# Low parts of weight units: by an accumulating DMA in place of a VectorE subtraction

## The chip, the cores and the metric

The kernel runs on one core of one Trainium2 chip. The metric is the device time of one execution in microseconds; times that a profile shows are microseconds from the start of the profiled execution's span.

## The reference, cut to what matters

Two layers of a bidirectional encoder over 1024 tokens of 1024 channels, in float32. Each layer norms its input, multiplies it by one input projection `w_in`, feeds the pieces to four mixers (Fourier, convolution, dilated attention, pooling), gates and projects each mixer's output, weights it by a sigmoid gate that is computed from the normed input, sums the four, and projects the sum by `w_out`.

```python
def hybrid_layer(x, ...):
    h = rms_norm(x, norm_g)
    z = h @ w_in                                   # 1024 x 4352
    u_a, u_b, u_c, u_d, u_gate = split(z)
    gate_paths = silu(u_gate)                      # one per mixer
    branch_outs = (fourier_mix(u_a, w_fourier), conformer_conv(u_b, ...),
                   dilated_mixture(u_c, cos, sin), multiscale_pool(u_d, ...))
    merged = 0
    for n, y in enumerate(branch_outs):
        y_n = (y * gate_paths[:, :, n]) @ w_branch[n]
        merged = merged + sigmoid(h @ w_gate[n] + b_gate[n]) * y_n
    return x + merged @ w_out
# out = rms_norm(layer 1(layer 0(x)))
```

## The kernel before

All activations lie transposed, channels on 128 partitions and tokens along the free axis, in two halves of 512 tokens. TensorE takes float32 operands rounded to a shorter format (`F32R`) in one pass, so every operand is split into a high and a low part, hi + lo = x exactly, and each product is the sum of three passes: hi hi, hi lo, lo hi (`passes`, L122; `together`, L249, where several units of weights share the right operand). A sum in PSUM takes its passes in order, so the third pass of its first block needs the low part of the weights.

Weights come in units of 1024 x 128 (512 KB). `load_unit` (L107) takes a raw place from the pool `wr` (L119, `raw`, two places for the whole kernel, the gate weights included), has SP load the unit into it, and calls `split` (L102): ScalarE copies the raw unit to the rounded high part (L104), VectorE subtracts that from the raw unit and writes the low part (L105). Both parts have places of their own: six halves under the tag `w`, which is three units, or places that are kept (tags `H` and `M`). The loads have a raised priority (`AHEAD` = 100 instructions), so that they run ahead of the products as far as places are free. A raw place is free again when both readers are done with it.

`load_unit` is called 135 times: for 75 units of `w_in` (attention, gate paths, mixers' inputs; `in_unit`, L325, with two halves of 24 products each; `begin`, L257, which in the first layer takes up to eight units at the start for one half of the tokens and loads some of them again later), 32 of `w_out` (`out_proj`, L1079), 16 of `w_branch` (`branch`, L922), and four each of `w_pool`, `w_pw` and `dft` in side work that is interleaved with the main products. The last layer's `out_proj` runs over the tokens in a half and two quarters: eight units for the half, eight for the third quarter (three of them loaded as kept copies during the half, five loaded then), and the last quarter with the kept eight.

`split` is also used for activations (`h`, attention probabilities, mixers' outputs) and, by `weight_form` (L961), for the gate weights' forms in the gate stages (`gates`, L1000), which don't call `load_unit`.

Instructions on each engine and each queue run in the order in which the tile framework's scheduler placed them when the program was built. SP issues nearly all DMAs: unit loads, the stores of branch products, the rotations' partition swaps in `rope_unit` (L353), the loads of x. POOL's queue issues the loads of branch products in the gate stages (L985) and the stores of merged blocks (L1062), and POOL does a few memsets.

Of the kernel before, what the change touches and what calls it, by code (L numbers as in the profile page):

```python
# [14 lines left out]
P = 128  # L15
# [23 lines left out]
# columns of the packed per-layer parameters  # L39
C_G, C_CW, C_CB, C_LG, C_LB, C_PS, C_BG, C_N = 0, 8, 70, 72, 74, 76, 78, 110  # L40
# columns of the packed constants
# [4 lines left out]
class Net:  # L46
# [41 lines left out]
    def half_pair(self, name, tag):  # L88
        """hi and lo of one [P, H] operand."""
        t = self.slot(name, F32R, tag=tag)  # L90
        return t[:, 0:H], t[:, H:S]
# [10 lines left out]
    def split(self, hi, lo, src):  # L102
        """hi + lo = src exactly, each part with few enough bits for one pass."""
        self.nc.scalar.activation(out=hi, in_=src, func=AF.Copy)  # L104
        self.nc.vector.tensor_tensor(out=lo, in0=src, in1=hi.bitcast(F32), op=ALU.subtract)  # L105

    def load_unit(self, src, kc=KC, n=P, tag=None, ahead=AHEAD):  # L107
        """A right shape of weights: hi and lo."""
# [5 lines left out]
        with self.tc.high_priority(offset=ahead):  # L114
            self.nc.sync.dma_start(out=flat, in_=src)
            self.split(*out, flat)
        return out

# [3 lines left out]
    def passes(self, ps, pairs, main=False, first=True, open_=False):  # L122
        """ps = sum over pairs of (lhsT hi, lo), (rhs hi, lo), in float32 by three passes.
        Not first: added to what ps holds. open_: ps is read between sums that add up in it."""
# [8 lines left out]
    def gemm(self, ps, w, x, hf, main=True):  # L133
        """x[k][hf]: hi and lo of the k-th 128 rows of the right operand, one half of the tokens."""
        self.passes(ps, [((w[0][:, k], w[1][:, k]), xk[hf]) for k, xk in enumerate(x)], main)

# [31 lines left out]
    def tok_stat(self, chunks, ones, name):  # L168
        """PSUM [token, 4 tiles, 2]: the mean over channels of the given [P, H] chunks' columns."""
# [24 lines left out]
    def spread(self, st, name):  # L194
        """[token, 4 tiles] to PSUM [P, H], the same in every partition."""
# [53 lines left out]
    def together(self, ws, xs, pss, ks=range(KC)):  # L249
        """Products that share their right operands."""  # L250
# [6 lines left out]
    def begin(self, units):  # L257
        """The first layer's first units. For the first of them and the first half of the tokens, x g is divided
        by the norms of its tokens after the products, which need not wait for them."""
# [70 lines left out]
    def first_units(self, l, units):  # L330
        """Their first halves of the tokens before the second ones, whose norm is still under way."""
# [8 lines left out]
    def perm_dst(self, ap, g, hf):  # L340
        """Where the tokens of half hf lie in group g's order."""
# [11 lines left out]
    def rope_unit(self, l, u, g, cos, sin, q):  # L353
        """The rotated unit, split and stacked, for each of the two heads (a: rows 0:64, b: rows 64:128).
        For k: hi over lo (a), lo over hi (b). For q: hi twice (a, b), and lo, both heads."""
# [40 lines left out]
    def v_tiles(self, vt, g, where):  # L396
        """v in the group's token order, tokens on partitions: hi, lo, rows by key offset."""
# [30 lines left out]
    def att_tiles(self, l, hp, g, q, k, vt, done):  # L428
# [18 lines left out]
        def products(t):  # L447
            # one bank per head: the two heads' products run in different rows of the array
# [70 lines left out]
        # scores of one tile, the transposes of the one before, the weighted sums of the one before that  # L519
# [30 lines left out]
    def att_mix(self, groups, park):  # L550
        """The groups' outputs weighted by the softmax of their log-sum-exps, parked in DRAM."""
# [72 lines left out]
    def pool_windows(self, c, up):  # L624
        """In place of u: its centred window mean less u."""
# [21 lines left out]
    def pool_mix(self, l, ups, gps, park):  # L647
        """The gated pooling branch, parked in DRAM until its merge."""
# [37 lines left out]
    def fourier_in(self, l, c):  # L686
        """The tokens folded twice, split. With a[n] = u[n] + u[S-n], s[n] = u[n] - u[S-n] and h = S/2, for n < S/4:
        a[n] + a[h-n] | a[n] - a[h-n] for the even and odd cosines, s[n] - s[h-n] | s[n] + s[h-n] for the sines.
        Aside: a[S/4], and the sum over all of u with alternating signs."""
# [35 lines left out]
    def fourier_pq(self, l, us, res):  # L725
        """P and Q: the transform over the channels and w_fourier, in one product each."""
# [72 lines left out]
    def gate_later(self, ys, gps, park):  # L799
        """The two chunks times their gate paths, once both are there, parked in DRAM."""  # L800
# [8 lines left out]
    def conv_units(self, l, c):  # L809
        """a times sigmoid(g), into DRAM between zeros."""  # L810
# [35 lines left out]
    def conv_mix(self, l, hf, gps, park):  # L846
        """Layer norm, SiLU, w_pw and the gate path of one half of the tokens, parked in DRAM."""
# [50 lines left out]
    def gated(self, load, gps, out):  # L898
        """Split halves of the two gated [P, S] chunks."""
# [34 lines left out]
    def token_forms(self, out):  # L934
        """The sums of h's blocks (b11 | b12 / b21 | b22: channels by tokens) for seven products in place of eight."""
# [30 lines left out]
    def spare(self, flip):  # L966
        """One more place for weights, two by turns."""
# [3 lines left out]
    def weight_forms(self, l):  # L971
        """In the order of the products: the weights' forms of all pairs of blocks, and what their merge needs."""
# [27 lines left out]
    def gates(self, l, tf):  # L1000
        """merged = sum over n of sigmoid(w_gate_n h + b_n) y_n, for two blocks of 128 channels at a time."""
# [263 lines left out]
```

## Time and profile before

| | us |
|---|---|
| median of 3 runs | 2097.05 (2096.38 to 2097.84) |
| span of the profiled execution | 2096.5 |
| what lies around the span, taken as the difference to the median | 0.55 |
| TensorE busy | 2023.1 |
| VectorE busy | 1487.6 |
| ScalarE busy | 1100.2 |
| POOL busy | 41.3 |

No time of the profiled execution is given apart from its span. In the profile PE is TensorE's products and PEld its loads of weights, which overlap; DVE is VectorE, ACT ScalarE, POOL GpSimd, and SPq and POOLq are the queues on which these two issue DMAs. A line such as L105 is that of `split`, whoever called it, so groups are told apart by the names of their tiles: `w<-wr` are the units of `load_unit`, `wf` the gate weights' forms. Idle time of an engine costs nothing by itself; what counts is which wait ends last in a stretch.

### The profile page before, as it was taken

The numbers are of one execution on the slowest core, as the hardware profiler recorded it, in microseconds if no ns is written. First come the engines' busy times: TensorE is split into PE (matmuls) and PEld (weight loads), VectorE is DVE, ScalarE is ACT, GpSimd is POOL, SyncE is SP. The second block draws the span as 40 slices with busy tenths as digits, with TensorE's granted clock in tenths as the row PEclk, the third lists the DMA queues.
The fourth block names the chain that finished last, engine by engine and source line by source line (L and its number), as shares of the span: only waits on it lengthen the run. The fifth ranks groups of instructions, "written<-read, shape, count | busy, mean of one in ns | idle before, by whom it ended". The sixth has DMA issues, their size and how long they took to land.

```text
span 2096.5 us, 26763 instructions
## 1 busy us (share of the span) xinstructions
PE 2023.1 (96%) x9500; PEld 1645.9 (79%) x9500; DVE 1487.6 (71%) x2752; ACT 1100.2 (52%) x2025; POOL 41.3 (2%) x90
## 2 busy tenths in 40 slices
PE   8998898999999999999999998989999999999998
PEld 6776686778878888887888776867888888888888
DVE  7596777775657877877655867687555867777775
ACT  7347666657755433434321566666685744344451
POOL 0000000000000000000000000000000000000000
PEclk9999998999999999999999999999999999999999
DMA  6231122212586234236421321223127843243443
GB/s 229 81 106 58 49 82 62 96 41 81 190 284 235 86 136 141 100 112 245 158 85 49 106 65 52 77 71 101 46 87 266 278 159 125 97 141 131 144 167 101
DMA packets 122438, 257.81 MB, mean 123 GB/s; under 512 B 31808, under 2 KB 36544, under 8 KB 122304
## 3 DMA queue, kind: packets, MB, share of 16 engines
q1 hardware_dynamic: 111360, 216.25, 31.1%
q0 software_dynamic: 10944, 39.85, 5.6%
q8 instruction: 75, 1.23, 0.2%
q14 instruction: 59, 0.48, 0.1%
HBM read 176.16 MB, written 67.30 MB: 116 GB/s over the span
## 4 chain that ended last, share of the span: by engine, by line
PE 73%; DVE 10%; ACT 9%; DMA 4%; issue 3%; SPq 1%; DVEq 0%; ACTq 0%
PE z L128 20%; PE ga L128 12%; PE g L128 8%; PE gb L128 8%; PE py L128 8%; PE op L128 6%; PE z L255 3%; DVE cv L841 2%; PE pv L128 2%; PE pt L486 1%; ACT p L474 1%; DVE w L105 1%; ACT qa L377 1%; ACT ql L383 1%; ACT qb L375 1%
## 5 line engine op out<-in xcount | busy, mean ns | idle before, releaser
L128 PE MATMUL z<-h,w 128*128 128x512 f32 x3000 | 760.9, 404 | 1.4 <-DVE gp L604 1.4
L128 PEld LDWEIGHTS z<-h,w 128*128 128x128 f32 x3000 | 557.0, 192 | 119.5 <-DVE gp L604 1.8
L104 ACT ACTIVATE w<-wr 128x1024 fp32r<-128x1024 f32 (+1 forms) x135 | 137.8, 1022 | 185.9 <-PE z L128 80.2
L105 DVE TENSOR_TENSOR w<-wr,w 128x1024 fp32r<-128x1024 f32 (+1 forms) x135 | 158.9, 1179 | 97.8 <-ACT w L104 81.6
L128 PE MATMUL ga<-t,wf 128*128 128x512 f32 x768 | 188.9, 395 | 0.0
L128 PE MATMUL gb<-t,wf 128*128 128x512 f32 x768 | 187.4, 393 | 0.0
L128 PE MATMUL g<-h,wf 128*128 128x512 f32 x768 | 186.3, 391 | 0.0
L128 PE MATMUL op<-m,w 128*128 128x512 f32 (+1 forms) x960 | 181.3, 349 | 2.0 <-DVE m L105 1.9
L128 PE MATMUL py<-g,w 128*128 128x512 f32 x768 | 181.5, 395 | 0.5 <-ACT y L930 0.5
L841 DVE SCALAR_TENSOR_TENSOR cv<-cv,params 128x512 f32<-128x512 f32 x240 | 178.9, 745 | 2.2
L128 PEld LDWEIGHTS op<-m,w 128*128 128x128 f32 x960 | 153.6, 189 | 28.0 <-DVE m L105 3.5
L128 PEld LDWEIGHTS ga<-t,wf 128*128 128x128 f32 x768 | 144.3, 188 | 33.6
L128 PEld LDWEIGHTS py<-g,w 128*128 128x128 f32 x768 | 143.3, 188 | 34.3 <-ACT y L930 1.7
L128 PEld LDWEIGHTS gb<-t,wf 128*128 128x128 f32 x768 | 144.3, 188 | 32.9
L128 PEld LDWEIGHTS g<-h,wf 128*128 128x128 f32 x768 | 144.2, 188 | 31.9
L104 ACT ACTIVATE wf<-wr 128x512 fp32r<-128x512 f32 x144 | 90.9, 632 | 130.4 <-issue 48.4
L105 DVE TENSOR_TENSOR wf<-wr,wf 128x512 fp32r<-128x512 f32 x144 | 98.8, 686 | 21.5 <-ACT wf L104 20.3
L474 ACT ACTIVATE p<-p,nm 128x192 f32<-128x192 f32 (+2 forms) x192 | 84.4, 441 | 54.0 <-DVE nm L471 53.6
L105 DVE TENSOR_TENSOR pl<-pt,ph 128x256 fp32r<-128x256 f32 (+2 forms) x136 | 63.2, 465 | 54.1 <-ACT ph L104 53.8
L104 ACT ACTIVATE wf<-s 128x512 fp32r<-128x512 f32 x64 | 40.4, 632 | 107.3 <-PE gb L128 64.4
L128 PE MATMUL ga<-h,wf 128*128 128x512 f32 x384 | 93.5, 392 | 0.0
L128 PEld LDWEIGHTS ga<-h,wf 128*128 128x128 f32 x384 | 72.1, 188 | 16.4
(246 smaller groups left out, 2832.4 us busy)
## 6 DMA issues: line engine op xcount, KB each, us to landing
wr<-in_w_in_dram SPq DMA_DIRECT2D x75, 512.0 KB, 3.7
y<-y SPq DMA_DIRECT2D x128, 256.0 KB, 3.8
y<-y POOLq DMA_DIRECT2D x64, 512.0 KB, 4.8
wr<-in_w_gate_dram SPq DMA_DIRECT2D x48, 512.0 KB, 4.4
wr<-in_w_out_dram SPq DMA_DIRECT2D x32, 512.0 KB, 3.6
rot<-rt SPq DMA_DIRECT2D x192, 64.0 KB, 2.0
cv<-in_w_gate_dram SPq DMA_DIRECT2D x16, 512.0 KB, 5.1
wr<-in_w_branch_dram SPq DMA_DIRECT2D x16, 512.0 KB, 5.0
```

The lines of the kernel that those rows point to most:

```text
L104: self.nc.scalar.activation(out=hi, in_=src, func=AF.Copy)
L105: self.nc.vector.tensor_tensor(out=lo, in0=src, in1=hi.bitcast(F32), op=ALU.subtract)
L128: self.nc.tensor.matmul(ps, w, x, start=(first and i + u == 0), stop=(i == n - 1 and u == 2), skip_group_check=open_)
L255: self.nc.tensor.matmul(ps, a[:, k], b, start=(k + j == 0), stop=(k == KC - 1 and j == 2))
L375: nc.scalar.activation(out=dst(x, own), in_=src(own), func=AF.Copy)
L377: nc.scalar.activation(out=dst(x, other), in_=src(own), func=AF.Copy)
L383: nc.scalar.activation(out=dst(xl, al), in_=src(al), func=AF.Copy)
L474: nc.scalar.activation(out=ph, in_=ph, func=AF.Exp, bias=nm[:, h:h + 1], accum_out=st[:, t, 2 + h:3 + h])
L486: nc.tensor.transpose(pt[:rows[ci], cs], p[:, off:off + rows[ci]], self.ident)
L841: self.tc.keep_in_program_order(nc.vector.scalar_tensor_tensor(out=y, in0=u[:, j:j + H], scalar=tap(j), in1=y, op0=ALU.mult, op1=ALU.add))
```

## The change

`load_unit` no longer calls `split`, but a new function. ScalarE copies the raw unit times -1, rounded, into the place of the low part. POOL issues a DMA that reads the raw unit and adds it to what stands in that place, so that it holds raw minus rounded raw. ScalarE copies the raw unit once more, into the high part. VectorE has no part in it. The order in the code is: negated copy, DMA, copy. All callers of `load_unit` are concerned, not only those of `w_in` and `w_out`; the other users of `split` are as before. The rest of the diff takes comments out.

```diff
         with self.tc.high_priority(offset=ahead):
             self.nc.sync.dma_start(out=flat, in_=src)
-            self.split(*out, flat)
+            self.split_by_dma(*out, flat)
         return out
+
+    def split_by_dma(self, hi, lo, src):
+
+        self.nc.scalar.activation(out=lo, in_=src, func=AF.Copy, scale=-1.0)
+        self.nc.gpsimd.dma_start(out=lo, in_=src, accum_op=ALU.add)
+        self.nc.scalar.activation(out=hi, in_=src, func=AF.Copy)
```

## Rows read from the trace of the kernel before

**Rows 1.** page, totals: busy us of each engine, share of the span, instructions

```profile
span 2096.5 us, 26763 instructions
PE 2023.1 (96%) x9500; PEld 1645.9 (79%) x9500; DVE 1487.6 (71%) x2752; ACT 1100.2 (52%) x2025; POOL 41.3 (2%) x90
```

**Rows 2.** stretches: from:to, length, busy us of each engine (instructions), clock, DMA share, GB/s

```profile
0.00:60.00 60.00, 52.04 (x222) 40.49 (x223) 46.01 (x73) 39.14 (x57) 0.49 (x10) 1.00 0.63 212
150.00:450.00 300.00, 274.64 (x1321) 217.92 (x1320) 222.12 (x514) 190.86 (x419) 0.00 (x0) 0.94 0.22 66
1150.00:1450.00 300.00, 276.18 (x1342) 221.39 (x1342) 226.91 (x479) 194.42 (x395) 0.00 (x0) 0.96 0.25 76
1580.00:1690.00 110.00, 110.00 (x490) 89.54 (x490) 70.23 (x109) 65.83 (x114) 3.18 (x6) 1.00 0.84 289
1975.00:2042.00 67.00, 65.59 (x301) 53.41 (x299) 46.99 (x62) 32.50 (x45) 0.00 (x0) 1.00 0.61 210
```

**Rows 3.** page, the chain that ended last, by engine and by line

```profile
PE 73%; DVE 10%; ACT 9%; DMA 4%; issue 3%; SPq 1%; DVEq 0%; ACTq 0%
PE z L128 20%; PE ga L128 12%; PE g L128 8%; PE gb L128 8%; PE py L128 8%; PE op L128 6%; PE z L255 3%; DVE cv L841 2%; PE pv L128 2%; PE pt L486 1%; ACT p L474 1%; DVE w L105 1%; ACT qa L377 1%; ACT ql L383 1%; ACT qb L375 1%
```

**Rows 4.** page, costliest groups: form, count | busy us, mean ns | idle before, releaser

```profile
L104 ACT ACTIVATE w<-wr 128x1024 fp32r<-128x1024 f32 (+1 forms) x135 | 137.8, 1022 | 185.9 <-PE z L128 80.2
L105 DVE TENSOR_TENSOR w<-wr,w 128x1024 fp32r<-128x1024 f32 (+1 forms) x135 | 158.9, 1179 | 97.8 <-ACT w L104 81.6
```

**Rows 5.** DMA issues: out<-in, queue, count, KB each, median us from issue to landing

```profile
wr<-in_w_out_dram SPq DMA_DIRECT2D x32, 512.0 KB, 3.6
y<-y POOLq DMA_DIRECT2D x64, 512.0 KB, 4.8
od<-o SPq DMA_DIRECT2D x12, 512.0 KB, 2.8
m<-y POOLq DMA_DIRECT2D x12, 512.0 KB, 6.9
```

**Rows 6.** page, the DMA queue that POOL issues on: packets, MB, share of 16 engines

```profile
q0 software_dynamic: 10944, 39.85, 5.6%
```

**Rows 7.** timeline of the last projection: start us, us, engine, line, form [idle before]

```profile
2000.88 1.06 ACT L104 ACTIVATE w<-wr 128x1024 fp32r<-128x1024 f32 x1 [2.66 <-PE op L128]
...
2017.23 1.06 ACT L104 ACTIVATE w<-wr 128x1024 fp32r<-128x1024 f32 x1 [0.44 <-DMA wr<-in_w_out_dram]
2018.32 1.23 DVE L105 TENSOR_TENSOR w<-wr,w 128x1024 fp32r<-128x1024 f32 x1 [0.81 <-ACT w L104]
2023.50 1.04 ACT L104 ACTIVATE w<-wr 128x1024 fp32r<-128x1024 f32 x1
...
2069.24 16.71 PE L128 MATMUL op<-m,w 128*128 128x256 f32 x138
```

**Rows 8.** timeline of the first layer's projection, two copies on ScalarE

```profile
1010.19 1.06 ACT L104 ACTIVATE w<-wr 128x1024 fp32r<-128x1024 f32 x1 [3.97 <-issue]
1015.70 1.06 ACT L104 ACTIVATE w<-wr 128x1024 fp32r<-128x1024 f32 x1 [3.92 <-issue]
```

**Rows 9.** timeline of the start

```profile
5.46 1.23 DVE L105 TENSOR_TENSOR w<-wr,w 128x1024 fp32r<-128x1024 f32 x1 [5.46 <-ACT w L104]
6.71 0.33 SPq L115 DMA_DIRECT2D wr<-in_w_in_dram  x1
7.09 1.42 SPq L246 DMA_DIRECT2D x<-in_xT_dram  x3
```

**Rows 10.** timeline where three units' places come free at once

```profile
73.85 1.06 ACT L104 ACTIVATE w<-wr 128x1024 fp32r<-128x1024 f32 x1 [7.83 <-PE z L255]
74.94 1.23 DVE L105 TENSOR_TENSOR w<-wr,w 128x1024 fp32r<-128x1024 f32 x1 [7.79 <-ACT w L104]
76.82 1.44 PE L128 MATMUL z<-h,w 128*128 128x512 f32 x5 [1.40 <-DVE gp L604]
```

**Rows 11.** waits of SP's DMA queue: who, for whom, us in all, times, longest

```profile
SPq L115 <- DVE w L105: 359.6, 81, 23.7
```

## The prediction

> **What bounds the kernel now.** I read the engine totals first: of a span of 2096.5 us TensorE is busy 2023.1, VectorE 1487.6, ScalarE 1100.2 [rows 1]. No change on VectorE or ScalarE can bring more than the 73 us in which TensorE is idle. Then the stretches [rows 2]: the two in which the attention units run hold 25 and 24 us of that idle time, with VectorE (222 and 227 of 300) and ScalarE (191 and 194) about equally loaded; the first 60 us hold 8; the branch products of the second layer have none, but a DMA share of 0.84; the last output projection has 1.4. Then the chain that ended last [rows 3]: TensorE is 73% of it, VectorE 10%, ScalarE 9%. The subtraction that goes (`DVE w L105`) is 1% of the chain, 21 us. So the reader should look for two things: how much of those 21 us is worth anything, and where a low part that comes later makes TensorE wait.
>
> **What goes and what comes.** All callers of `load_unit` change: 135 units [rows 4]: 75 of w_in, 32 of w_out, and 28 of w_branch, dft, w_pw and w_pool. VectorE loses 135 x 1.179 = 159 us. ScalarE gains a second pass over each unit; no row has a copy with a scale of -1 of this shape, so I price it as its neighbour, the rounding copy: 135 x 1.022 = 138 us (an estimate). POOL gets 135 issues and the DMA engines 135 transfers that read 512 KB from `wr`, read 512 KB of the low part and write it back.
>
> The decisive number is the time from the end of the negated copy to the landing of the accumulating DMA; call it L. No row shows an accumulating DMA. Rows near it [rows 5]: a 512 KB store from SBUF, issued by SP, lands in 2.8 us; a 512 KB load issued by POOL in 4.8; a 512 KB store issued by POOL in 6.9. An accumulation reads its destination too. What one more pass over 512 KB costs follows from POOL's queue [rows 6]: 39.85 MB took 5.6% of the span, 117 us, for 76 transfers, 1.5 us each. So L lies between 2.8 (SP's store, nothing added) and 6.9 + 1.5 = 8.4. I take 4.8 + 1.5 = 6.3, nearest to the POOL load, because it too writes SBUF and is issued by the same queue. Until now the low part was there 1.23 us after the high part [rows 7].
>
> The Trainium skill, DMA: Bandwidth & Descriptors, section Anatomy of one DMA, fits a POOL-issued DMA as 2.0 us plus bytes over 436 GB/s, which would be 3.2 us here; by it the sum below would have almost no term left but the start. The POOL row of 4.8 us for a plain load disagrees with that fit already. The skill's Collectives: The Full Stack, section The bandwidth ceiling, says that a DMA reduction pays for two source reads and not for the adding; the trace has no reduction to test it, and it agrees with adding one pass.
>
> **Why L costs time although units are loaded ahead.** `load_unit` has two raw places (`wr`) for all units, and three units' worth of places (`w`, 6 halves). A raw place is free again only when its last reader is done: today the subtraction, then the accumulating DMA. Two loads take one turn of the two places. At the end of the last projection that turn is visible [rows 7]: the copy of one unit starts at 2017.23 and that of the unit two loads later at 2023.50, 6.27 us, of which VectorE's part is 1.23. After the change the turn is 6.27 - 1.23 + L = 5.04 + L, 11.3 us at L = 6.3, so 5.7 us a load.
>
> Last projection. It makes 16 loads: eight units for the first half of the tokens, three kept copies, and five more for the third quarter. The fourth load's copy starts at 2000.88 because its place was freed then by TensorE [rows 7]; from there 12 loads are six turns: the 16th low part is there at 2000.9 + 1.1 + L + 6 x (5.04 + L) = 2032.2 + 7L. After it TensorE still has that unit and the eight of the last quarter, 2.9 us each (138 products take 16.71 us, a unit is 24) [rows 7], so 26.2 us. The last product ended at 2085.95. The delay is 2032.2 + 7L + 26.2 - 2086.0 = 7L - 27.6 us: +16.5 at L = 6.3, +31 at 8.4, and none below 3.9. This is the largest term.
>
> First layer's projection: a unit takes 5.5 us (copies at 1010.19 and 1015.70) [rows 8], two take 11.0 and the turn 11.3. Eight turns run 2.6 us over, and a place is freed 11 us before its unit is needed while its low part takes 1.1 + 6.3, so 3.6 us of lead cover it: I take +1; at 8.4 the turn is 2.4 us too long, eight times, less 1.5 of lead: up to +18.
>
> Start. The first subtraction ends at 6.69 and releases SP's third weight load at 6.71; three loads of x stand behind it on SP from 7.09 [rows 9]. With the accumulation the first raw place is free at 5.4 + L = 11.7, so that load and these x come 5 us later, and the first sums use every x and cannot be made up later: +5. Then, at 73.9, the places of three units come free at once; today the next unit is split by 76.2 and TensorE goes on at 76.82 [rows 10]. Its low part would be there at 74.9 + 6.3 = 81.2: +4.5. ScalarE's ten more copies in the first 60 us (39 busy) [rows 2] I cost at nothing, since it has 21 us free; if it is full at the wrong moment they cost up to 5. Start +9.5; at 2.8 about +2, at 8.4 +14 and those 5.
>
> Attention stretches, 36 units of queries, keys and values (18 a layer). VectorE is relieved by 1.2 us a unit and ScalarE loaded by 1.0, at nearly equal loads [rows 2]; beside the 21 us of chain the subtraction has, the new copy takes a place on ScalarE's queue ahead of the copies of queries, keys and probabilities. Bounds -10 (half of the 21 us pays) and +10; I take 0. SP's queue counts too: SP already waits 359.6 us, 81 times, for a subtraction before a weight load [rows 11]; each such wait grows by L - 1.2 = 5 us, and behind it stand the rotations' DMAs of `rope_unit`. I cost that at 0, because a raw load is queued one to two units ahead; without that cover it is the third rival below.
>
> Branch products, eight units a layer: each new transfer is 2 x 1.5 us of all engines, eight are 24 us in 110, so a DMA share of 0.84 becomes 1.06 [rows 2]: at most 7 us a layer, and TensorE has two units of weights in hand there; I take +2 for both layers. In the gate stages `load_unit` isn't called, and POOL's y loads stand beside no accumulation except at their edges: 0.
>
> **Sum.** 16.5 + 1 + 9.5 + 0 + 2 = +29. The profiled span of 2096.5 lies 0.55 under the median of 2097.05; I carry those 0.55 along: 2097 + 29 = 2126 us. With every term at its lower bound it is -10 + 2 = 2089, with every term at its upper 31 + 18 + 19 + 10 + 14 = +92, 2189.
>
> **Rivals.** First, faster: L is short, near SP's 2.8 us store [rows 5], say under 3.9. Then the last projection's term is zero, and the relief of VectorE decides in the attention stretches: -10 + 2, about 2089; with no relief 2099. For it: the transfer stays in SBUF, and VectorE is on the chain as much as ScalarE. Against it: no POOL row is under 4.8. The skill's fit named above would be this case. Chance 0.17, of which 0.10 faster by over 0.2%. Second: the accumulation is much slower than a copy with one more read, L near 12 us, because its read and its write of the same bytes don't overlap. The last projection then loses 7 x 12 - 27.6 = 56, the first eight turns of 6.0 = 48 less nothing, the start 20: +124, 2221. For it: no row shows how such a transfer runs; against it: all 512 KB rows lie within 2.8 and 6.9. Chance 0.14. Third: L is as forecast, but SP stops in front of the rotations: by their share of the units (36 of 135) 22 of the 81 waits lie there; half of them on the chain is 11 x 5 = 55, half of which the lead covers, so +28 on top: 2154. Chance 0.10. That the change does not do what it says can't show in the time: it would be a low part of other bits.
>
> **How the numbers follow.** The forecast, 2126, has 0.59; its own range with L from 4.8 to 8.4 is 2105 to 2175. 0.2% of this time, 4 us, is about what a measurement of this kernel can tell from no change. Faster: 0.10 from the first rival. Same: 0.07 from it and 0.03 from forecasts with L near 4.5. Slower: 0.56 + 0.14 + 0.10 = 0.80. The range for 8 in 10 is 2092 to 2195: it leaves out the best of the first rival and most of the second.
>
> **What would show it.** Right: accumulating DMAs that land about 6 us after their issue; in the last projection copies of weights two loads apart by 11 us and TensorE idle in front of `op`; a gap in TensorE at about 80 us; SP's wait for weight loads up by several hundred us; VectorE at about 1330 us, ScalarE at 1240. Wrong: landings under 4 us with an unbroken `op` stretch, or ScalarE waiting for DMAs in the attention stretches, or TensorE gaps there that exceed the ones I place at both ends.

## The result and the profile after

The changed kernel takes 2215.66 us (median of four runs, 2206.39 to 2219.19), the kernel before 2097.45 beside it: a ratio of 1.0553, 95% interval 1.0523 to 1.0582. The forecast was 2126, the range 2092 to 2195; the loss of 118 us is four times the 29 that I summed up. The profiled run took 2206.39 us with a span of 2204.6; against the profile of before that is 108 us, and the sections below share out these 108.

The page's totals and the chain that ended last, of the kernel after (as [rows 1] and [rows 3]):

```profile
span 2204.6 us, 27110 instructions
PE 2061.8 (94%) x9500; PEld 1663.6 (75%) x9500; DVE 1344.8 (61%) x2617; ACT 1211.2 (55%) x2156; POOL 157.6 (7%) x225
...
PE 47%; DMA 17%; issue 13%; ACT 12%; DVE 9%; SPq 1%; POOL 0%; DVEq 0%; ACTq 0%; POOLq 0%
PE ga L134 11%; PE z L134 9%; PE g L134 8%; PE gb L134 7%; DMA w<-wr 6%; PE py L134 4%; PE op L134 3%; DMA wr<-in_w_in_dram 3%; DVE cv L847 3%; DMA wr<-in_w_out_dram 2%; PE pv L134 1%; ACT w L121 1%; DMA rot<-rt 1%; ACT p L480 1%; ACT qa L383 1%
```

VectorE lost 143 us of work and ScalarE gained 111 (159 and 138 were summed up). But TensorE's share of the chain fell from 73% to 47%, and DMAs rose from 4% to 17%. TensorE does the same 9500 products in 39 us more: of the 108 us, 39 are products that take longer and 69 are more idle time.

The new work, from the page of after: POOL's queue, the negated copy and the issue (count | busy, mean ns | idle before), and the issue-to-landing median (as [rows 4 to 6]):

```profile
q0 software_dynamic: 30384, 107.75, 21.9%
...
L121 ACT ACTIVATE w<-wr 128x1024 fp32r<-128x1024 f32 (+1 forms) x135 | 137.8, 1021 | 212.0 <-DMA wr<-in_w_in_dram 55.6
L122 POOL DMA_DIRECT2D w<-wr x135 | 116.5, 863 | 1422.9 <-ACT w L121 1288.8
...
w<-wr POOLq DMA_DIRECT2D x127, 512.0 KB, 5.2
```

Waits of SP's queue in after (as [rows 11]: us in all, times, longest):

```profile
SPq L115 <- DMA w<-wr: 632.6, 110, 25.5
```

Waits of ScalarE in after, the same columns:

```profile
ACT w L121 <- DMA wr<-in_w_in_dram: 55.6, 15, 7.7
ACT w L121 <- DMA wr<-in_w_out_dram: 53.9, 15, 6.6
```

SP stands longer at raw loads, and the negated copy waits 110 us for raw loads that come late; before, the copy in its place waited 15 us for them. The negated copy costs what a copy costs, 1021 ns. The accumulating DMA lands 5.2 us after its issue begins, and the issue follows the negated copy by 0.3, so L is 5.5 us in the median. It isn't the same everywhere: taken unit by unit, the median is 4.9 us in the attention stretches, 6.5 in the last projection and 6.7 in the branch products, and the longest is 10.4. From POOL's queue, 21.9% of 2204.6 us less the 117 of the other transfers [rows 6], it holds all 16 engines for 2.8 us a whole unit (127 whole ones, four halves and four eighths make 129.5). Both were forecast (6.3 and 3.0). So the parts were priced right, and the sum was still wrong by a factor of four.

Where the time went, by stretches, in the kernel before. Columns: from:to, length, busy us of TensorE, its weight loads, VectorE, ScalarE and POOL (instructions), granted clock, DMA share, GB/s. The stretches are the start up to the first transposes of v, the branch products of layer 0, the first layer's output projection, the branch products of layer 1, and the last projection; each starts at the first product of its kind.

```profile
0.00:145.37 145.37, 135.44 (x583) 107.82 (x583) 107.23 (x157) 73.32 (x107) 0.49 (x10) 1.00 0.45 145
561.50:656.75 95.25, 94.70 (x418) 76.11 (x416) 61.86 (x97) 58.83 (x104) 3.31 (x6) 1.00 0.82 285
963.87:1055.51 91.64, 90.41 (x398) 73.11 (x396) 60.97 (x88) 39.67 (x57) 0.29 (x4) 1.00 0.54 186
1590.56:1684.44 93.88, 93.88 (x418) 76.35 (x416) 59.87 (x93) 59.40 (x104) 3.18 (x6) 1.00 0.81 280
1991.47:2096.50 105.03, 94.08 (x601) 84.29 (x599) 65.00 (x122) 34.96 (x57) 0.00 (x0) 0.97 0.40 135
```

The same stretches in the kernel after:

```profile
0.00:173.47 173.47, 142.98 (x582) 112.63 (x583) 83.39 (x134) 92.58 (x130) 20.42 (x33) 0.96 0.71 184
595.85:706.66 110.81, 98.85 (x418) 78.36 (x416) 56.74 (x92) 66.46 (x114) 8.40 (x12) 0.95 0.90 283
1016.55:1115.83 99.28, 94.50 (x396) 75.01 (x397) 42.93 (x72) 54.20 (x73) 13.48 (x20) 0.97 0.94 254
1662.75:1769.06 106.31, 98.00 (x417) 77.21 (x416) 56.24 (x91) 65.71 (x113) 8.40 (x12) 0.97 0.89 287
2079.05:2204.60 125.55, 101.04 (x600) 87.86 (x600) 50.71 (x110) 49.94 (x73) 12.01 (x14) 0.92 0.67 180
```

These five lost 28.1, 15.6, 7.6, 12.4 and 20.5 us, 84 of the 108. In each, TensorE's busy time went up with the same products, and its clock went down.

### The profile page after: what moved, and what is told of

It reads as the page before. It is cut to its first block, busy times and chain, and to the rows that moved or that the text cites. A ratio compares the mean times of both kernels' runs of the same rounds, so it can differ in the third digit from the quotient of the medians.

```text
span 2204.6 us, 27110 instructions
## 1 busy us (share of the span) xinstructions
PE 2061.8 (94%) x9500; PEld 1663.6 (75%) x9500; DVE 1344.8 (61%) x2617; ACT 1211.2 (55%) x2156; POOL 157.6 (7%) x225
## 3 DMA queue, kind: packets, MB, share of 16 engines
q0 software_dynamic: 30384, 107.75, 21.9%
## 4 chain that ended last, share of the span: by engine, by line
PE 47%; DMA 17%; issue 13%; ACT 12%; DVE 9%; SPq 1%; POOL 0%; DVEq 0%; ACTq 0%; POOLq 0%
PE ga L134 11%; PE z L134 9%; PE g L134 8%; PE gb L134 7%; DMA w<-wr 6%; PE py L134 4%; PE op L134 3%; DMA wr<-in_w_in_dram 3%; DVE cv L847 3%; DMA wr<-in_w_out_dram 2%; PE pv L134 1%; ACT w L121 1%; DMA rot<-rt 1%; ACT p L480 1%; ACT qa L383 1%
## 5 line engine op out<-in xcount | busy, mean ns | idle before, releaser
L134 PE MATMUL z<-h,w 128*128 128x512 f32 x3000 | 769.7, 407 | 8.6 <-ACT cg L827 4.9
L121 ACT ACTIVATE w<-wr 128x1024 fp32r<-128x1024 f32 (+1 forms) x135 | 137.8, 1021 | 212.0 <-DMA wr<-in_w_in_dram 55.6
L122 POOL DMA_DIRECT2D w<-wr x135 | 116.5, 863 | 1422.9 <-ACT w L121 1288.8
L134 PE MATMUL op<-m,w 128*128 128x512 f32 (+1 forms) x960 | 192.6, 361 | 21.9 <-DMA w<-wr 15.1
L134 PE MATMUL py<-g,w 128*128 128x512 f32 x768 | 189.7, 405 | 20.3 <-ACT y L936 19.2
L134 PEld LDWEIGHTS op<-m,w 128*128 128x128 f32 x960 | 158.9, 195 | 54.3 <-DMA w<-wr 19.1
L134 PEld LDWEIGHTS ga<-t,wf 128*128 128x128 f32 x768 | 144.3, 188 | 33.8
L123 ACT ACTIVATE w<-wr 128x1024 fp32r<-128x1024 f32 (+1 forms) x135 | 136.7, 1012 | 7.0 <-PE gb L134 3.5
L105 DVE TENSOR_TENSOR wf<-wr,wf 128x512 fp32r<-128x512 f32 x144 | 98.8, 686 | 22.3 <-ACT wf L104 21.2
```

Of the source, the lines that this page charges most:

```text
L121: self.nc.scalar.activation(out=lo, in_=src, func=AF.Copy, scale=-1.0)
L122: self.nc.gpsimd.dma_start(out=lo, in_=src, accum_op=ALU.add)
L134: self.nc.tensor.matmul(ps, w, x, start=(first and i + u == 0), stop=(i == n - 1 and u == 2), skip_group_check=open_)
```

## The experiments

The table puts them side by side: us by which a stretch is longer than in the kernel before, from the profiled runs. "Between" are the input units from the Fourier product to the branch products; both layers are added up.

| stretch | changed kernel | no_transfer | plain_copy | latency_alone | traffic_alone | three_raw | latency_three_raw |
|---|---|---|---|---|---|---|---|
| start | 28.1 | 3.2 | 14.6 | 31.0 | 8.9 | 27.6 | 27.9 |
| attention | 7.1 | 4.8 | -0.5 | -2.1 | 13.5 | 10.5 | 3.4 |
| between | 9.9 | 0.9 | 5.8 | 13.0 | 8.6 | 12.8 | 11.8 |
| branch products | 28.0 | 2.7 | 16.4 | 12.4 | 20.4 | 25.1 | 19.5 |
| gate stages | 5.7 | 0 | 1.7 | 3.8 | 0 | 6.1 | 0 |
| first projection | 7.6 | -1.7 | 2.6 | 13.2 | 3.7 | 5.0 | 7.3 |
| from there to the second layer's v | 1.1 | 0.3 | 0.2 | 4.8 | 0 | 1.2 | 1.4 |
| last projection | 20.5 | -0.4 | 9.5 | 27.1 | 26.4 | 21.2 | 19.6 |

Theory A was the forecast's: the raw places are held until a transfer lands, and the turn of the two of them sets the pace. Rival B: ScalarE's second pass. Rival C: the bytes of the transfers.

**Without the transfer, and with a plain copy.**

```diff
-        self.nc.gpsimd.dma_start(out=lo, in_=src, accum_op=ALU.add)
```

> The changed kernel without the accumulating DMA: ScalarE writes the negated copy and the copy, VectorE has no part in it, and the low part stays the negated rounded part (so this kernel leaves out the addition of the raw unit). It tells ScalarE's second pass and VectorE's relief apart from the transfer. Theory A (the time goes into the turn of the two raw places, which holds the landing of the transfer): a raw place is free about 2.1 us after the load, as before, so nearly all of the +118 us is gone: 2085 to 2105 us, last projection and start within 5 us of before. Rival B (ScalarE's second pass in an engine queue that runs in order costs the time): at least a third of the loss stays, 2135 us or more, in the branch products and the start.

Measured: 2105.74 us, ratio 1.0045 (1.0029 to 1.0062). Rival B falls as the main cause. ScalarE's pass does cost some 9 us more than the relief of VectorE brings, with no accumulating DMA at all: the 143 us that VectorE is busy less don't make up for it. (No run has the relief without the second pass, so what it is worth alone isn't shown.)

```diff
-        self.nc.gpsimd.dma_start(out=lo, in_=src, accum_op=ALU.add)
+        self.nc.gpsimd.dma_start(out=lo, in_=src)
```

> The changed kernel with a plain copy by the same queue in place of the accumulating DMA (what is left out: the addition; the low part is the raw unit). Theory A (turn of the raw places): the time follows the landing. If the plain copy lands only 0.5 us sooner than the median of 5.1 us, the last projection gives back 7 x 0.5 = 3.5 us and the whole kernel 5 to 15: about 2205. Rival C (the bytes of the transfers crowd out the other transfers): the read of the destination goes away, so the 2.7 us of all DMA engines for each unit becomes about 1.5 and over 40% of the loss goes, 2165 us or less, even where landings hardly change.

Measured: 2147.17 us, ratio 1.026 (1.023 to 1.029). POOL's queue and the landing, from its page:

```profile
q0 software_dynamic: 30384, 107.75, 14.5%
...
w<-wr POOLq DMA_DIRECT2D x127, 512.0 KB, 3.5
```

It holds the engines for 1.5 us a unit (14.5% of 2146.7 us, less 117, over the same 129.5 units) and lands in 3.5, 1.7 sooner than the accumulating one. More than half of the loss goes. Both quantities fall together here, so this run doesn't choose between A and C.

**A third raw place.** The control first, then the place on top of it.

```diff
-NH, NM, NA, NT = 16, 8, 11, 12
+NH, NM, NA, NT = 16, 8, 11, 10
```

> The changed kernel with ten in place of twelve temporary places (NT), which frees the room that a third raw place needs; control for three_raw. All theories: within 1% of the changed kernel, 2195 to 2240 us.

Measured: 2208.01 us, ratio 1.0538 (1.0522 to 1.0553): the temporary places make no difference.

```diff
-        return self.wp.tile([P, KC, P], F32, tag="wr", name="wr", bufs=2)
+        return self.wp.tile([P, KC, P], F32, tag="wr", name="wr", bufs=3)
```

> The changed kernel with three raw places in place of two, and ten temporary places. Theory A (turn of the two raw places): the turn of two loads of 10.5 to 12 us becomes a turn of three loads of the same length, 3.5 to 4 us a load, less than the 5.7 us in which TensorE uses a unit. Last projection +20 becomes +5 or less, start +28 becomes about +15, branch products +28 become +10 or less: 2130 to 2165 us, if the control is near 2216. Rivals B (ScalarE's second pass) and C (bytes): as slow as the control, within 15 us.

Measured: 2205.26 us, ratio 1.0526 (1.0511 to 1.0542): nothing gained. The expectation failed clearly. Its last projection, in three stretches of 10 us (columns as above):

```profile
2110.00:2120.00 10.00, 7.13 (x25) 5.36 (x24) 1.29 (x2) 3.47 (x5) 0.86 (x1) 0.83 0.98 238
2120.00:2130.00 10.00, 7.19 (x25) 5.39 (x24) 2.58 (x4) 5.58 (x7) 2.58 (x3) 0.83 0.99 225
2130.00:2140.00 10.00, 9.62 (x51) 7.92 (x50) 2.67 (x4) 5.05 (x6) 1.72 (x2) 1.00 1.03 232
```

With three places the DMA engines are full (share 0.98 to 1.03), and the negated copies come in threes, 11 to 14 us apart: a load in some 4.8 us (eight from 2104.42 to 2142.83) where the changed kernel takes 5.5 (eight from 2104.00 to 2148.04).

**Bytes without the wait, and wait without the bytes.** traffic_alone is the kernel before, with ten temporary places and this:

```diff
             self.split(*out, flat)
+            aside = self.aside[:, :kc * n].rearrange("p (k n) -> p k n", n=n)
+            self.nc.gpsimd.dma_start(out=aside, in_=out[0].bitcast(F32), accum_op=ALU.add)
```

> The kernel before, with its subtraction on VectorE, and after each unit's split one accumulating DMA of the same size by POOL's queue that adds the high part to a place of its own which nobody reads (ten in place of twelve temporary places make the room). The bytes of the change without its wait: no raw place and no low part hangs on it. Theory A (the time goes into waits on the landing): 2095 to 2112 us, since the kernel before takes 2095. Rival C (the bytes crowd the DMA engines, so that the raw loads and the stores land later): at least half of the +118 us, 2150 us or more, with raw loads landing in 4 us and more. If both meet, that is if the transfers make a turn long only where the turn already holds the transfer, it lies between, 2110 to 2140.

Measured: 2180.52 us, ratio 1.0401 (1.0378 to 1.0425).

latency_alone is the changed kernel with this:

```diff
-        self.nc.gpsimd.dma_start(out=lo, in_=src, accum_op=ALU.add)
+        for _ in range(2):
+            self.nc.gpsimd.dma_start(out=lo[:, 0:1], in_=src[:, 0:1], accum_op=ALU.add)
```

> The changed kernel, but in place of one accumulating DMA of a whole unit two of an eighth of it, one after the other onto the same columns (what is left out: the addition on the other columns, and it is made twice on these). The wait of the change without its bytes: two landings of small transfers, 2.4 us and more each with 0.9 us of issue, hold the raw place for about 6 us, as the whole transfer does with its median of 6.4. Theory A: as slow as the changed kernel within 25 us, 2185 us or more. Rival C: the kernel without the transfer takes 2106, so 2105 to 2130. If both meet, between: 2130 to 2180.

Measured: 2203.44 us, ratio 1.0511 (1.0486 to 1.0535). Either alone costs most of the loss, and the two don't add up. Neither is pure, though. In latency_alone the wait is longer than the one that it stands for: from the end of the negated copy to the second landing it is 6.7 us in the median, in the changed kernel 5.4 (in the start 7.2 against 5.6, in the branch products 8.9 against 6.7). And its small transfers still take time of the DMA engines; POOL's queue, from its page:

```profile
q0 software_dynamic: 49824, 59.14, 12.6%
```

Less the 117 us of the other transfers that is 1.2 us a unit, not far from the plain copy's 1.5, for a good quarter of its bytes. In traffic_alone the transfers queue up behind each other on POOL, and since they read the high parts, ScalarE waits for a weights' place: 40.9 us in 8 places, of which two with 17.4 us lie in the last projection and three with 8.9 in the start. Its 26.4 us in the last projection are no price for bytes. So the table shows to which side a stage leans, not two prices: the start to the wait (31.0 against 8.9), the branch products to the bytes (12.4 against 20.4).

**The stores of the branch products by ScalarE's queue.**

```diff
-                    self.nc.sync.dma_start(out=self.y[l][n, 4 * u + dd, :, hf * H:hf * H + H], in_=y)
+                    self.nc.scalar.dma_start(out=self.y[l][n, 4 * u + dd, :, hf * H:hf * H + H], in_=y)
```

> The changed kernel with the stores of the branch products issued by ScalarE's queue, right behind the copy that writes them, in place of SP's. Theory D (in the branch products the stores stand on SP behind a raw load that waits for a landing, so the copies out of PSUM and TensorE wait): the +28 us of the two branch stages fall to 14 or less, 2190 to 2205 us. Without it: 2207 to 2222, and TensorE waits for the copies of y as before.

Measured: 2218.81 us, ratio 1.0578 (1.0553 to 1.0603); the branch stages lie 32 us over before, no less than without it, so the gain that theory D forecast isn't there. But the waits are other ones: TensorE's waits for the copies of y fell from 19.2 us to 9.8, and 8.2 us of waits for low parts stand in their place. Moving the stores is worth nothing; that they had no part in the waits isn't shown.

**The subtraction on GpSimd.**

```diff
-        self.nc.scalar.activation(out=lo, in_=src, func=AF.Copy, scale=-1.0)
-        self.nc.gpsimd.dma_start(out=lo, in_=src, accum_op=ALU.add)
         self.nc.scalar.activation(out=hi, in_=src, func=AF.Copy)
+        self.nc.gpsimd.tensor_tensor(out=lo, in0=src, in1=hi.bitcast(F32), op=ALU.subtract)
```

> Not the change but its aim by another means: ScalarE copies the high part as before the change, and GpSimd makes the subtraction that VectorE made, with no DMA and no second pass on ScalarE. No trace shows what this subtraction takes on GpSimd. A turn of two raw loads is 5.04 us and that time: under 6 us it stays under the 11 us in which TensorE uses two units, and then the relief of VectorE decides: 2085 to 2100 us. Over 6 us the turn binds as with the DMA, and the time is 2130 us or more; it would also be slower if GpSimd's reads and VectorE's hinder each other, which would show in VectorE's mean durations.

Measured: 2213.52 us, ratio 1.0546 (1.0521 to 1.0571). As slow as the change, but with the largest loss elsewhere: the attention stretches lose 52 us (341.3 and 348.4 against 322.8 and 315.0), the branch products 26. It is taken up under the hardware below.

**One part at a time.** `load_unit` gets an argument that chooses between `split` and `split_by_dma`; one caller at a time sets it.

```diff
-            self.split_by_dma(*out, flat)
+            (self.split_by_dma if dma else self.split)(*out, flat)
```

> The kernel before with the change in `begin` alone (the first layer's first units), all other units split as before. In the changed kernel the stretch to the first transposes of v lost 28 us. In latency_alone, which has the wait without the bytes, it lost 31, in traffic_alone, which has the bytes without the wait, 9. Theory A for the start (each raw place is held until the landing, and the next load and the loads of x behind it on SP come later): 20 to 30 us here too, 2115 to 2128 us. Rival: the stretch loses because of the units after `begin` too, or because ScalarE and SP run far ahead into work that the change has delayed: under 15 us.

> The change in the 16 units of `w_branch` alone. In the changed kernel the two branch stages lost 15.6 and 12.4 us, in latency_alone 4.4 and 8.0, in traffic_alone 11.6 and 8.9. Theory C for this stage (eight more transfers of 2.7 us of all DMA engines where the share was 0.82 already): 20 to 28 us, 2116 to 2126 us, and a DMA share of 0.88 or more in the stage. If it is mostly work that arrives late from the stages ahead: under 12 us.

> The change in the 32 units of `w_out` alone. The changed kernel lost 20.5 us in the last projection and 7.7 in the first layer's. If the stages are independent, 25 to 31 us, 2120 to 2130 us; the forecast's terms for them were 16.5 and 1. With the turn of two loads near 11 us in the last one.

> The change in the units of `w_in` outside `begin` alone (attention, gate paths, mixers' inputs). The forecast costed them at nothing, between -10 and +10. What the changed kernel lost outside the start, the branch stages and the projections is 118 - 28 - 28 - 28 = about 34 us, of which the profiled run shows 7 in the attention stretches, 10 in the Fourier and gate-path units behind them, 6 in the gate stages. If the loss lies in these units themselves: 20 to 35 us, 2117 to 2132 us. If it comes from work that is late from elsewhere, -5 to +10 us.

Measured: 2121.66, 2131.16, 2135.09 and 2118.85 us, ratios 1.0115 (1.0098 to 1.0132), 1.0157 (1.013 to 1.0185), 1.0178 (1.0161 to 1.0196) and 1.0102 (1.0086 to 1.0118). The four gains over 1 sum to 0.055, the whole change's 0.055 (the 12 units of side work are in none of the four): in total the parts add up. In the profiles each loss lies in the part's own stretches: start 24.6 us; branch products 33.8; last projection 19.8, first 9.5 and gate stages 6.5; attention 7.9, between 7.3 and start 5.0. Stage by stage the sums fit less well: the branch products lose 33.8 us alone and 28.0 within the whole change. only_branch and only_out cost more than expected, only_start and only_in lie in their ranges.

**What is left in the branch products and at three places.**

latency_three_raw has the edits of latency_alone and of three_raw:

> latency_alone (two small accumulating DMAs, one after the other, in place of the whole one; the addition on the other columns is left out) with three raw places and ten temporary places. It differs from three_raw in the bytes alone. Theory F (two limits: the turn of the raw places and the bytes; either is enough in the projections and in the start): here both are lifted, so the last projection falls from +27 us to under 8, the first layer's from +13 to under 4, the start from +31 to under 16: 2110 to 2145 us. Rival E (the landing itself is late for the first sums, whatever the places): 2180 us or more, as latency_alone.

Measured: 2188.61 us, ratio 1.0429 (1.0407 to 1.045). 91 us stay, and the start keeps 27.9 of 31: there TensorE waits 14.6 us in four places for low parts, so with a third place too the landing comes too late. For the projections the run doesn't decide about theory F, because it brings a limit of its own. In the last projection raw loads now go out 4.2 to 4.7 us apart, and that is the pace of POOL's queue, as its rows there show:

```profile
2081.71 1.75 POOL L123 DMA_DIRECT2D w<-wr  x2 [2.76 <-DMA w<-wr]
```

These two issues are the second small transfer of a unit, which waits until the first has landed, and right behind it the first of the next unit, whose negated copy is done by then. In the kernel before the copies of loads 8 to 13 of that stage come 2.95 us apart (2017.23 to 2031.99, five steps), and TensorE needs them so.

branch_latency is only_branch with the edit of latency_alone, branch_raw_by_pool is only_branch with the raw loads of w_branch on POOL's queue, raw_by_pool the changed kernel with all of them there:

```diff
-            self.nc.sync.dma_start(out=flat, in_=src)
+            self.nc.gpsimd.dma_start(out=flat, in_=src)
```

> only_branch, but with two small accumulating DMAs, one after the other, in place of the whole one (the addition on the other columns is left out). only_branch lost 34 us, all in the two branch stages. Theory C for this stage (the whole transfers stand beside the loads of the parked branches, which land in 5 to 9 us in place of 4): the loss falls to under 12 us, 2100 to 2109 us. Rival A (SP and ScalarE wait for landings at the two raw places): 20 us and more stay, 2117 us or more.

Measured: 2118.05 us, ratio 1.0094 (1.0077 to 1.011). With a good quarter of the bytes the stage still loses 21.8 of the 33.8 us; but the second landing comes 8.8 us after the negated copy in the median, in only_branch 6.5, so this is no price for the same wait. How it loses them, its timeline shows (start us, us, engine, line, form [idle before]):

```profile
596.78 0.86 POOL L123 DMA_DIRECT2D w<-wr  x1 [1.79 <-DMA w<-wr]
...
602.44 0.33 SPq L115 DMA_DIRECT2D wr<-in_w_branch_dram  x1
602.87 0.38 SPq L925 DMA_DIRECT2D unpark<-att  x1
...
608.37 0.63 ACT L104 ACTIVATE g<-gt 128x512 fp32r<-128x512 f32 x1 [3.45 <-DVE gt L916]
...
609.85 0.58 ACT L937 ACTIVATE y<-py 128x512 f32<-128x512 f32 x1
...
610.48 27.61 PE L135 MATMUL py<-g,w 128*128 128x512 f32 x107 [5.96 <-ACT y L937]
```

SP stands at the raw load until the transfer of 596.78 has landed; the load of a parked branch goes out behind it at 602.87; VectorE's product, ScalarE's copy g and, behind g in the same queue, the copy of y out of PSUM follow; TensorE, whose next product writes a place that this copy frees, waits 5.96 us.

> only_branch, with the raw loads of the 16 units of w_branch issued by POOL's queue, ahead of their accumulating DMAs, in place of SP's. Theory G (SP stands at a raw load until the accumulation of two units before lands, and the loads of the parked branches, and then the copies of g and y on ScalarE, stand behind it): the loss falls from 34 to 8 to 18 us, 2105 to 2115 us; the rest is the bytes. Rival (ScalarE's order and the bytes): 2125 us or more.

Measured: 2123.85 us, ratio 1.0124 (1.0107 to 1.0141); the stage still loses 30.2. Taking the raw loads off SP's queue brings little, and by the timeline the chain is then held up at another load:

```profile
1628.19 0.54 POOL L115 DMA_DIRECT2D wr<-in_w_branch_dram  x1 [6.26 <-DMA w<-wr]
1628.44 0.78 SPq L590 DMA_DIRECT2D og<-od  x1
1628.72 0.91 POOL L122 DMA_DIRECT2D w<-wr  x1
...
1640.75 0.63 ACT L104 ACTIVATE g<-gt 128x512 fp32r<-128x512 f32 x1 [8.87 <-DVE gt L915]
...
1649.40 30.05 PE L134 MATMUL py<-g,w 128*128 128x512 f32 x119 [10.10 <-ACT y L936]
```

The load of og goes out between a raw load and an accumulating DMA of 512 KB each; VectorE's step on it starts at 1637.48 only (put down there to a store; at the same place in only_branch to this load, after 8.41 us). In the stage the loads of og take 5.5 us in the median, before the change 4.0. The same chain over g and y then stops TensorE for 10.10 us.

> The changed kernel with all raw loads of load_unit issued by POOL's queue in place of SP's. Theory G: start +28 falls to 10 to 20 (the loads of x no longer stand behind a raw load), branch stages +28 to 12 or less, the projections stay at +20 and +8 or lose some more, since a raw load by POOL lands later than one by SP and stands in one queue with the accumulations: 2165 to 2195 us. If SP's order doesn't matter: 2205 us or more.

Measured: 2259.19 us, ratio 1.0772 (1.0756 to 1.0789), slower still. The start keeps its 29 us, but that doesn't clear SP's order: POOL's queue now holds raw loads and accumulating DMAs in turn, and the third raw load goes out at 17.96, later than SP's at 14.42 in the changed kernel. The gate stages lose nothing any more (-0.1). The attention stretches go from +7.1 to +23, and the first projection goes from +7.6 to +36, because POOL now stands at raw loads (377 us in 84 waits for `w<-wr`) with the accumulating DMAs behind them.

## Why the prediction was wrong, step by step

Of the 79 us that the sum missed, 26 lie in the branch products, where it followed the wrong chain, 19 in the start, where it followed one turn of three, 10 in units that weren't in it at all, and only 4 in the last projection, its largest term.

**L and the engines' time per transfer**: right, 5.5 us and 2.8 against 6.3 and 3.0. In the last projection, for which I used it, L is 6.5. The rival of a short L falls with that. The second rival forecast nearly the right total, 2221, but its cause, a landing near 12 us, is not there.

**Last projection, +16.5 against +20.5**: the mechanism was right, the sum 4 us short. Timeline of after (as [rows 7]):

```profile
2104.00 1.06 ACT L121 ACTIVATE w<-wr 128x1024 fp32r<-128x1024 f32 x1 [1.87 <-DMA wr<-in_w_out_dram]
...
2114.55 1.06 ACT L121 ACTIVATE w<-wr 128x1024 fp32r<-128x1024 f32 x1 [5.18 <-DMA wr<-in_w_out_dram]
...
2123.57 7.14 PE L134 MATMUL op<-m,w 128*128 128x512 f32 x24 [4.08 <-DMA w<-wr]
...
2127.67 1.06 ACT L121 ACTIVATE w<-wr 128x1024 fp32r<-128x1024 f32 x1
...
2135.40 7.71 PE L134 MATMUL op<-m,w 128*128 128x512 f32 x24 [4.70 <-DMA w<-wr]
...
2167.70 6.42 PE L134 MATMUL op<-m,w 128*128 128x256 f32 x52 [0.73 <-DMA w<-wr]
```

The stretch of the same projection right behind the gap of 4.70 us (columns as for the stretches above):

```profile
2136.00:2140.00 4.00, 4.00 (x11) 3.13 (x10) 0.00 (x0) 3.00 (x4) 0.86 (x1) 0.50 0.58 169
```

The turn of two loads is 10.55 us in the timeline and 11.0 in the mean of the eight loads from 2104.00 to 2148.04; 11.3 was forecast. The end hangs on the 16th low part, as forecast: TensorE goes on with it at 2167.70, 88.7 us after the stage's start where my sum gives 84.8, and 26.3 us pass from there to the end of the last `op` product (26.2 forecast). What was short is mainly the fourth load's copy (2090.42, 11.4 us into the stage and not 9.4) and the six turns (69.5 us and not 68.0).

What I didn't ask is when the earlier low parts are needed. The kept copies are loaded ahead of units 5, 6 and 7 of the first half, so these units stand 7th, 9th and 11th in the loads, two loads to one unit of products: there TensorE needs a load every 2.95 us, and it waits 1.97, 4.08 and 4.70 us at their third passes. The 11th load (copy at 2127.67, low part at 2135.40) is 56.4 us after the stage's start; before, TensorE was at that product after some 40. So it is 16 us late there already, and waits only 0.73 us more for the 16th. Two limits end almost together, and that the one I looked at gives nearly the right number is in part luck.

**The clock**: missing from the sum altogether. In the row above, right after the idle 4.70 us, the granted clock is 0.50, the lower level of 1.2 GHz, and the 24 products from 2135.40 take 7.71 us where the branch stage of only_branch has rows of 24 such products in 5.81 at a clock of 1.00. TensorE's busy time rose by 7.0 us in the last projection, 4.2 and 4.1 in the branch stages, 4.1 in the first projection, 7.5 in the start, 39 in all: beside each us of new idle time stands over half a us of slower products. That is no price yet. In the last projection the slower products add nothing to the end, since TensorE still comes 0.73 us before the 16th low part. I read [rows 2] with clocks of 0.94 to 1.00 and never asked what new gaps would do to them. Whether the lower clock lies wholly behind the gaps wasn't tried by itself.

**Start, +9.5 against +28.1**: I followed one turn of the raw places; three lie in its first 45 us. Before, the third, the fifth and the seventh raw load went out at 6.71, 15.55 and 22.22; SP's rows after (as [rows 9]) and the products beside them:

```profile
5.77 1.00 POOL L122 DMA_DIRECT2D w<-wr  x1 [4.74 <-ACT w L121]
...
14.39 0.80 PE L261 MATMUL z<-cv,w 128*128 128x512 f32 x1 [4.99 <-DMA w<-wr]
14.42 0.33 SPq L115 DMA_DIRECT2D wr<-in_w_in_dram  x1
...
29.05 0.80 PE L261 MATMUL z<-cv,w 128*128 128x512 f32 x1 [4.27 <-DMA w<-wr]
29.05 0.33 SPq L115 DMA_DIRECT2D wr<-in_w_in_dram  x1
```

The first landings take longer (8.6 us for the first, beside the loads of x), and the delay grows from 7.7 us at the third load to 13.5 at the fifth and 19.2 at the seventh (41.40). The x that I placed behind the third raw load now go out ahead of it, by 6.95, so they don't wait for it, and in three_raw a third place leaves 27.6 us of the loss. What is there is waits for low parts: 15.8 us of TensorE's time in six places, before the change none. So it is mainly the landing in front of sums that need it at once. The gap that I placed at about 80 us is at 97.7 after, with 3.35 us, and is put down to another copy on ScalarE.

**Branch products, +2 against +28**: the largest error. I checked the cover of the weights, two units, and that held: TensorE waits for no low part there. What I left out is that the stage's tight chain is another one: loads of the parked branches, VectorE's product, the copy g, the copy y, all over SP's and ScalarE's queues in order. It had little room: before, ScalarE already sat 6.03 us in front of a copy g, without a gap in TensorE.

```profile
1625.47 0.63 ACT L104 ACTIVATE g<-gt 128x512 fp32r<-128x512 f32 x1 [6.03 <-DVE gt L909]
```

I named the share of 0.84 that would become 1.06 and took 2 us of the up to 14. Measured by itself it is 34 us: 22 stay with a good quarter of the bytes (and a longer wait), 25 to 30 with the raw loads off SP's queue. So the two overlap, and how the loss splits between the wait and the bytes stays open.

**First projection, +1 against +7.6**: mis-sized, and mostly not in the term that I had. The turns in only_out are 11.2 to 12.8 us, not 11.3, but TensorE waits only 1.6 us for low parts in the changed kernel; 2.8 us go to a step of the next layer's norm on VectorE, and 4.1 are slower products. What made that step late wasn't tried.

**Gate stages, 0 against +5.7**: the edge that I excepted in words and didn't price. At the stage's end SP stands at a raw load of w_out until a landing, and the loads of the merged blocks, `mt`, go out behind it; ScalarE's copy of them, and with it the first product of the projection, comes late:

```profile
1011.29 2.80 SPq L1078 DMA_DIRECT2D mt<-m  x6
...
1016.55 0.50 PE L134 MATMUL op<-m,w 128*128 128x512 f32 x1 [2.69 <-ACT m L104]
```

only_out has this loss (6.5), and raw_by_pool, where `mt` doesn't stand behind a raw load, has none: so here the loads that stand behind SP's raw load are the cause.

**Attention, 0 against +7.1**: inside the bounds of 10; no_transfer has 4.8 of it without the accumulating DMA. The third rival, SP in front of the rotations, would have added 28 here and didn't, though SP's waits did grow from 359.6 to 632.6 us. **Between, not in the sum, against +9.9**: only_in has 7.3 there; I never priced these units.

## What to carry to other kernels

Price a new latency in each stage by the load that is needed soonest there as well as by the last one, not by the mean alone, and let it run through every turn of the buffers. Where an in-order queue feeds several chains (SP's loads, ScalarE's copies), look for the tightest chain of the stage, even if it has nothing to do with the operand that changes, and see what idle time it already hides. Look at what the lower clock behind a gap of TensorE costs, and before any of this try what the change is worth without its price: here the relief of VectorE with ScalarE's second pass cost 0.45% before any DMA. And measure in a control what it is meant to keep: the two small transfers that stood for the wait made it longer and still held the DMA engines.

## What the runs showed of the hardware

Taking the accumulation out of a 512 KB transfer by POOL brings its landing from 5.2 to 3.5 us, its hold on the DMA engines from 2.8 to 1.5 us and its issue on POOL from 0.86 to 0.53. The hold doesn't follow the bytes: the two small transfers of latency_alone, a good quarter of a unit's bytes, hold the engines for 1.2 us. The Trainium skill's DMA: Bandwidth & Descriptors, section Anatomy of one DMA, gives an estimate of 3.2 us for any such transfer (2.0 us plus bytes over 436 GB/s): the plain copy here agrees within 0.3, the accumulating one doesn't.

With GpSimd's subtraction VectorE's operations take longer. GpSimd's line in gpsimd_sub, with durations in ns, min/median/max:

```profile
L122 POOL TENSOR_TENSOR w<-wr,w x135: 467/2407/11365, 5.5 to 2157.7; 128x1024 fp32r<-128x1024 f32 x127, 128x128 fp32r<-128x128 f32 x4, 128x512 fp32r<-128x512 f32 x4
```

Two groups of VectorE in gpsimd_sub, by line (busy us, mean ns | idle before):

```profile
L846 DVE SCALAR_TENSOR_TENSOR cv<-cv,params 128x512 f32<-128x512 f32 x240 | 213.3, 889 | 2.6
L215 DVE TENSOR_TENSOR acc<-acc,sq 128x512 f32<-128x512 f32 (+1 forms) x49 | 64.1, 1309 | 31.5 <-ACT sq L214 30.9
```

The same two groups in the kernel before:

```profile
L841 DVE SCALAR_TENSOR_TENSOR cv<-cv,params 128x512 f32<-128x512 f32 x240 | 178.9, 745 | 2.2
L210 DVE TENSOR_TENSOR acc<-acc,sq 128x512 f32<-128x512 f32 (+1 forms) x49 | 30.0, 612 | 8.0 <-ACT sq L209 7.3
```

It takes 2.4 us in the median, twice VectorE's 1.18 [rows 4], and up to 11.4. Of VectorE's own operations several groups grow, one from 612 to 1309 ns in the mean, so that its busy time stays at 1491 us with 159 us of work taken away. The Trainium skill's GPSIMD Engine Reference, section 1. Specifications, says that GpSimd's access to SBUF is shared with VectorE and contends with its instructions of two SBUF inputs; these rows agree.
